# Four tile pairs of each FFN up projection computed by seven half-size products, with the residual kept in DRAM meanwhile

## The chip, the cores and the metric

The kernel runs on one core of a Trainium2 chip. The metric is device time in microseconds (us) of one execution. Engines are named as in the profile: PE (TensorE products), PEld (its weight loads), DVE (VectorE), ACT (ScalarE), POOL (GpSimd) and SP (SyncE, which here only issues DMAs).

## The reference

The reference is an encoder trunk of four layers over x of 512 tokens by 1024 channels, in float32. Each layer is a token mixer (a convolution module, a 2-D neighbourhood attention, a bidirectional retention, and the convolution module again) followed by a gated FFN with a depthwise convolution over tokens. Both are residual. The FFN is what the change touches:

```python
FFN_DIM = ((8 * D_MODEL // 3 + 127) // 128) * 128        # 2816 = 22 * 128

def conv_ffn(h, w_up, dw_w, dw_b, w_down):
    u = dwconv(h @ w_up, dw_w, dw_b)                      # w_up: 1024 x 5632, dwconv: 3 taps
    val, gate = jnp.split(u, 2, axis=-1)
    return (jax.nn.gelu(gate) * val) @ w_down             # w_down: 2816 x 1024

h = rmsnorm(x, norm2_g[i])
x = x + conv_ffn(h, ffn_w_up[i], ffn_dw_w[i], ffn_dw_b[i], ffn_w_down[i])
```

## The kernel before

Activations lie with channels on the partitions: x is eight tiles `x[k]` of 128 channels x 512 tokens, resident in SBUF. For float32 accuracy each operand of a product is split into a high and a low part of the fast format (`split`, `split_w`: a cast on ACT, then a subtraction on DVE), and each product is three (`mm3`, lines 178 to 181: high by high, high by low, low by high). Weights stream from DRAM on the SP queue into two raw buffers (`wraw`), and are split into three high and three low buffers (`whi`, `wlo`).

The four FFNs are `ffn(l, after)`, each in these steps:

- **Up.** The 44 output tiles of 128 channels come as 22 pairs: tile n = 2j is value tile j, n = 2j + 1 is gate tile j. `up(n)` makes one in one PSUM bank: 8 channel tiles x 3 products = 24 products of 128 x 128 weights by 512 tokens. The odd tiles in `ACC` get the low part of their weights by an accumulating DMA on POOL instead of DVE (`load_w_acc`), and have their products on lines 307, 308 and 312.
- **Scaling.** The first tiles use unscaled x. When the norm's statistics are known (after tile `S2[l]`), `scale_first` writes x * gain * rstd into eight temporaries `xs` (line 331), and after tile `SCALED[l] - 1` `scale_rest` splits them anew into `xhi`, `xlo`, which the later tiles read.
- **Middle.** `mid(j)` applies the three taps (lines 349 to 353), the gelu and the gate product. Of pairs below 16 each two channel tiles and the two token halves of 256 make seven combinations `F` (lines 372 to 378), split into `Hh`, `Hl`; pairs 16 to 21 stay plain.
- **Down.** For pairs 0 to 7 and 8 to 15 `down` makes, for each two output tiles, seven products with sums of weight blocks in place of eight with the blocks, each over four channel tiles: 84 products of 256 columns. This is a group, four to each half. `weights` makes the sums with a broadcast load, an accumulating DMA on POOL (line 422) and DVE additions. Two half banks are copied to a temporary `s12` on ACT (lines 467, 470); the results go into the residual `x` in SBUF (line 471 by DMA, lines 473, 476, 454 on DVE). A group's last two products (`finish`) come after the next group's first five, or after the up tiles of the next pair.
- **Rest.** `down_rest` adds pairs 16 to 21 by plain products and finishes `x[o]` (line 292), on which the next mixer starts.

Temporaries `t512` rotate through a pool of `NT_FFN` = 9 tiles. Each engine runs its own instructions in a fixed order, which a scheduler with a timing model lays out when the kernel is built, from the order of the program; so neighbouring up tiles may interleave on PE. DMAs from one engine are issued in that order too.

Of the kernel before, what the change touches and what calls it, by code (L numbers as in the profile page):

```python
# [8 lines left out]
F32 = mybir.dt.float32  # L9
F32R = mybir.dt.float32r  # L10
I32 = mybir.dt.int32
AF = mybir.ActivationFunctionType
# [5 lines left out]
P = 128  # L18
T = 512
D = 1024  # L20
# [51 lines left out]
PART_COL = (0, 2048)  # L72
REST = 16
SLOT_H = 4
NT_FFN = 9
NWS = 3
SCALED = (5, 7, 5, 5)
ACC = tuple(n for n in range(3, 2 * FT, 2) if n // 2 not in (8, 9, 16, 17))


@with_exitstack
def tile_trunk(
# [1 line left out]
    tc: tile.TileContext,  # L84
    xT, par, cos, sin, nmask, rel,
    cw_in, cdw, cdb, cw_out, nat_qkv, rpb, nat_out,
    ret_qk, ret_v, ret_g, ret_out, f_up, f_down, f_rest,
    out,
):
    nc = tc.nc  # L90
# [9 lines left out]
    def nm(s):  # L100
        uid[0] += 1
        return f"{s}{uid[0]}"
# [38 lines left out]
    def pc(name, i=0, w=1):  # L141
        c = COLS[name] + i
        if c < 64:
            return png[:, c:c + w]
        return pt[:, c:c + w]
# [81 lines left out]
                ps[:, b * P:(b + 1) * P], col[:, b:b + 1].broadcast_to([P, P]), ident)  # L227

    state = {"late": [], "squares": []}

    @contextmanager
    def behind(*names):
# [61 lines left out]
    def ffn(l, after):  # L294
        with ExitStack() as st:
# [23 lines left out]
                    scale_rest()  # L319
                return ps  # L320

            xs = []

            def scale_first():
                if SCALED[l] > 2 * FT:
                    return
                for tag in ("Hh0", "Hl0", "Hh1"):
                    t = hp.tile([P, 7, 256], F32, tag=tag, name=nm("xs")).rearrange("p a b -> p (a b)")
                    xs.extend(t[:, i * T:(i + 1) * T] for i in range(3))
                for k in range(KD):  # L330
                    nc.vector.scalar_tensor_tensor(
                        xs[k], x[k], pc("n2g", l * 8 + k), rstd_bc, MUL, MUL)

            def scale_rest():
                for k in range(KD):
                    split(xs[k], xhi[k], xlo[k])

            H, rest, cur_f = {}, {}, {}

# [69 lines left out]
                    state["spare"] = spare  # L409
                return pss  # L410

            def weights(i, q, gate=None):
                p0, p1 = PARTS[q]
                n, c = (p1 - p0) * P, PART_COL[q]
                src = f_down[l, i]
                r13 = hp.tile([P, D], F32, tag="ws", name=nm("ws"), bufs=NWS)
                sg = hp.tile([P, D], F32, tag="wq", name=nm("wq"))
                with tc.issue_after(gate.ins) if gate else ExitStack():
                    nc.sync.dma_start(
                        r13[:, :2 * n].rearrange("p (b n) -> p b n", b=2),  # L420
                        src[:, c + 2 * n:c + 3 * n].unsqueeze(1).broadcast_to([P, 2, n]))
                    nc.gpsimd.dma_start(r13[:, :2 * n], src[:, c:c + 2 * n], accum_op=ADD)
                    r1 = load_raw(src[:, c:c + 2 * n], 2 * n)
                    nc.sync.dma_start(sg[:, n:2 * n], src[:, c + 3 * n:c + 4 * n])
                w1 = split_w(r1, 2 * n, nc.vector)
                w13 = split_w(r13, 2 * n, nc.vector)
                r2 = r13[:, n:2 * n]
                nc.vector.tensor_tensor(r2, r2, r1[:, :n], ADD)
                h2 = hp.tile([P, T], F32R, tag="h2", name=nm("h2"))
                l2 = hp.tile([P, T], F32R, tag="l2", name=nm("l2"))  # L430
                split(r2, h2[:, :n], l2[:, :n])
                nc.vector.tensor_tensor(sg[:, :n], r2, sg[:, n:2 * n], ADD)
                h4 = hp.tile([P, D], F32R, tag="h4", name=nm("h4"))
                l4 = hp.tile([P, D], F32R, tag="l4", name=nm("l4"))
                split(sg[:, :2 * n], h4[:, :2 * n], l4[:, :2 * n])
                u = lambda w, b: (w[0][:, b * n:(b + 1) * n], w[1][:, b * n:(b + 1) * n])
                return {"a11": u(w1, 0), "a22": u(w1, 1), "s3": u(w13, 0), "s1": u(w13, 1),
                        "s2": u((h2, l2), 0), "sg": u((h4, l4), 0), "a12": u((h4, l4), 1)}

            def prod(o, w, q, b, start, stop=True, part=None):  # L440
                p0, p1 = PARTS[q]
                for p in part or range(p0, p1):
                    s = slice((p - p0) * P, (p - p0 + 1) * P)
                    hi, lo = H[p]
                    mm3(o, w[0][:, s], w[1][:, s], hi[:, b, :], lo[:, b, :],
                        start and p == p0, stop and p == p1 - 1, True)

            def down(q, first, late, filler):
                p0, p1 = PARTS[q]

                def finish(i, w, v, s12):
                    prod(v[:, :256], w["sg"], q, 2, False)
                    prod(v[:, 256:], w["a12"], q, 3, True)
                    nc.vector.tensor_tensor(x[2 * i + 1], v, s12, ADD)

                prev = None
                for i in range(4):
                    w = weights(i, q) if i else first
# [8 lines left out]
                    nc.scalar.copy(s12[:, 256:], xc)  # L467
                    prod(v[:, 256:], w["a22"], q, 6, True, part=now)
                    prod(xc, w["s2"], q, 0, False)
                    nc.scalar.copy(s12[:, :256], xc)  # L470
                    nc.gpsimd.dma_start(s12, x[2 * i + 1], accum_op=ADD)
                    prod(v[:, :256], w["s1"], q, 4, True)
                    nc.vector.tensor_tensor(x[2 * i], x[2 * i], v, SUB)
                    prod(xc, w["s3"], q, 5, False)
                    xh2 = x[2 * i].rearrange("p (h t) -> p h t", h=2)
                    nc.vector.tensor_tensor(
                        xh2, xh2, xc.unsqueeze(1).broadcast_to([P, 2, 256]), SUB)
# [41 lines left out]
                    after(o)  # L519

            ups = up_first()
            done, n = 0, 2

            def mids(upto):
                nonlocal done
                while done < upto:
                    for _ in mid(done, ups[2 * done], ups[2 * done + 1]):
                        pass
                    done += 1

            def ups_of(j):
                nonlocal n
                while n < 2 * j + 2:
                    ups.append(up(n))
                    n += 1

            starts = {2 * p1 + (l == 1 and q == 0): q for q, (_, p1) in enumerate(PARTS)}
            for j in range(1, FT):
                ups_of(j)
                w0 = weights(0, starts[j], state["load"]) if j in starts else None  # L540
                if n > S2[l]:
                    mids(j)
                if w0:
                    down(starts[j], w0, lambda: mids(j + 1), lambda: ups_of(j + 1))
            mids(FT)
            state["sq"] = nc.vector
            down_rest()
            del state["sq"]
# [645 lines left out]
                        pair_wout(pss, 3, o2, y3)  # L1194

    def nat_bias():
        dram = ctx.enter_context(
            tc.tile_pool(name="dram", bufs=1, space=bass.MemoryType.DRAM))
# [82 lines left out]
def _layout(inp):  # L1281
# [67 lines left out]
    rw = f["ret_w_in"][0]  # L1349
    rv = rw[:, 2048:4096].reshape(4, 2, P, 4, 512).transpose(3, 0, 2, 1, 4)  # L1350
    rout = f["ret_w_out"][0].reshape(4, 4, P, 4, 2, P).transpose(0, 3, 2, 4, 1, 5)
    fd = f["ffn_w_down"].reshape(4, FT, P, 8, P)
    macros = []
    for i in range(4):
# [22 lines left out]
        "ret_g": tiles(rw[:, 4096:]),  # L1377
        "ret_out": rout.reshape(4, 4, P, D),
        "f_up": tiles(f["ffn_w_up"]),
        "f_down": fdown,  # L1380
        "f_rest": frest,
    }
# [19 lines left out]
```

## Time and profile before

| | |
|---|---|
| median of 3 runs | 2552.09 us (2547.99 to 2552.65) |
| the profiled execution: own time | 2553.76 us |
| its span in the trace | 2552.0 us |
| granted PE clock, mean | 0.997 |
| instructions | 36973 |
| 212 to 549 us, most of the first FFN: PE / DVE / ACT / POOL busy | 336.6 / 215.9 / 163.6 / 45.4 of 337 us |
| the same for 830 to 1160 us, most of the second | 329.9 / 220.2 / 167.3 / 39.1 of 330 us |
| DMA in the whole run | 341.21 MB, 134 GB/s on average |

A profile row by line gives: line, engine, operation, output<-input, shapes, count | busy us, mean ns of one | idle time of the engine just before such instructions, and what ended it. A timeline row gives start, duration, engine, line, and in brackets the idle time before it. Matmuls overlap in the pipeline, so their pace is read from the distance of their starts, not from their listed duration.

### The profile page before, as it was taken

The page shows a single profiled execution, that of the slowest core. Times are in us where ns is not written, and L with a number is a line of the kernel's source. Part 1 is how long each engine was busy: PE and PEld are TensorE (multiplying, and loading weights), DVE is VectorE, ACT ScalarE, POOL GpSimd, SP SyncE. Part 2 cuts the span into 40 slices and gives each one's busy share as a digit, 9 for nine tenths or more (in the row PEclk, how much of TensorE's full clock was granted, in tenths as well). Part 3 has the DMA queues.
Part 4 walks back from the last instruction along what each step waited for, and adds up shares of the span by engine and source line. Part 5 has one row for each costly group of instructions (what it writes and reads, how often), then busy time and mean ns, then how long its engine had stood idle before and what let it go on. Part 6 is the DMA issues. An engine that isn't in the chain of part 4 may idle for free.

```text
span 2552.0 us, 36973 instructions
## 1 busy us (share of the span) xinstructions
PE 2531.0 (99%) x14590; PEld 2158.3 (85%) x14590; DVE 1737.3 (68%) x2828; ACT 1215.1 (48%) x1635; POOL 342.5 (13%) x412
## 2 busy tenths in 40 slices
PE   9999999999999999999999999999999999999999
PEld 7888898979998888888888888889898888789897
DVE  7976766667877676656666565677575887676664
ACT  5454544454656555444332423454444445454442
POOL 1214010003421210100000000200000121100000
PEclk9999999999999999999999999999999999999999
DMA  7725757534232565653222222475754572475653
GB/s 244 233 75 172 178 136 175 139 101 119 81 93 82 131 176 143 171 131 112 82 81 68 84 76 67 114 177 129 183 130 110 203 225 74 115 181 133 177 136 107
DMA packets 107903, 341.21 MB, mean 134 GB/s; under 512 B 13345, under 2 KB 16289, under 8 KB 107729
## 3 DMA queue, kind: packets, MB, share of 16 engines
q1 hardware_dynamic: 81856, 264.72, 33.9%
q0 software_dynamic: 24576, 71.41, 14.9%
q10 hardware_dynamic: 1296, 2.72, 0.3%
q8 instruction: 114, 1.87, 0.3%
q14 instruction: 61, 0.49, 0.1%
HBM read 321.00 MB, written 5.63 MB: 128 GB/s over the span
## 4 chain that ended last, share of the span: by engine, by line
PE 92%; DVE 4%; DMA 2%; ACT 1%; issue 1%; SPq 0%; DVEq 0%; ACTq 0%
PE ps L180 21%; PE ps L179 21%; PE ps L181 21%; PE ps L312 5%; PE ps L308 5%; PE ps L307 5%; PE ps L184 3%; PE ps L186 3%; PE ps L185 3%; DMA wr<-in_f_down 1%; PE ps L665 1%; PE ps L664 1%; PE ps L663 1%; PE ps L400 1%; PE ps L405 1%
## 5 line engine op out<-in xcount | busy, mean ns | idle before, releaser
L165 ACT CAST wh<-wr 128x1024 fp32r<-128x1024 f32 (+1 forms) x310 | 318.2, 1028 | 548.2 <-PE ps L180 204.6
L166 DVE TENSOR_TENSOR wl<-wr,wh 128x1024 fp32r<-128x1024 f32 (+1 forms) x307 | 371.4, 1210 | 231.2 <-ACT wh L165 170.9
L180 PE MATMUL ps<-xl,wh 128*128 128x512 f32 x1312 | 520.3, 397 | 0.3 <-DVE xl L249 0.3
L179 PE MATMUL ps<-xh,wh 128*128 128x512 f32 x1312 | 518.1, 396 | 1.0 <-ACT wh L165 1.0
L181 PE MATMUL ps<-xh,wl 128*128 128x512 f32 x1312 | 516.9, 395 | 0.1
L179 PEld LDWEIGHTS ps<-xh,wh 128*128 128x128 f32 x1312 | 246.3, 188 | 61.7 <-ACT wh L165 1.8
L181 PEld LDWEIGHTS ps<-xh,wl 128*128 128x128 f32 x1312 | 246.3, 188 | 59.2 <-DVE wl L166 0.5
L180 PEld LDWEIGHTS ps<-xl,wh 128*128 128x128 f32 x1312 | 246.4, 188 | 57.7 <-DVE xl L249 0.6
L180 PE MATMUL ps<-Hl,wh 128*128 128x256 f32 (+1 forms) x734 | 224.4, 307 | 1.1 <-DVE Hl L190 1.0
L179 PE MATMUL ps<-Hh,wh 128*128 128x256 f32 (+1 forms) x734 | 223.2, 306 | 0.0
L181 PE MATMUL ps<-Hh,wl 128*128 128x256 f32 (+1 forms) x734 | 222.7, 307 | 0.1
L307 PE MATMUL ps<-xh,wh 128*128 128x512 f32 x544 | 215.1, 395 | 0.0
L308 PE MATMUL ps<-xl,wh 128*128 128x512 f32 x544 | 214.9, 395 | 0.0
L351 DVE SCALAR_TENSOR_TENSOR t<-ps,par,t 128x511 f32<-128x511 f32 x154 | 114.8, 746 | 143.3 <-ACT t L349 143.3
L184 PE MATMUL ps<-wh,xh 128*128 128x256 f32 (+1 forms) x512 | 159.5, 314 | 2.0 <-DVE x L505 2.0
L186 PE MATMUL ps<-wh,xl 128*128 128x256 f32 (+1 forms) x512 | 159.9, 313 | 0.0
L185 PE MATMUL ps<-wl,xh 128*128 128x256 f32 (+1 forms) x512 | 159.6, 313 | 0.0
L175 POOL DMA_DIRECT2D wl<-in_f_up x68 | 59.8, 879 | 665.4 <-ACT wl L174 539.9
L180 PEld LDWEIGHTS ps<-Hl,wh 128*128 128x128 f32 x734 | 138.2, 188 | 9.5 <-DVE Hl L190 1.7
L181 PEld LDWEIGHTS ps<-Hh,wl 128*128 128x128 f32 x734 | 137.5, 188 | 8.9 <-DVE wl L166 1.8
L179 PEld LDWEIGHTS ps<-Hh,wh 128*128 128x128 f32 x734 | 137.7, 188 | 7.7
L312 PE MATMUL ps<-xh,wl 128*128 128x512 f32 x544 | 137.8, 395 | 0.0
(298 smaller groups left out, 5463.5 us busy)
## 6 DMA issues: line engine op xcount, KB each, us to landing
wr<-in_f_up SPq DMA_DIRECT2D x176, 512.0 KB, 4.0
wl<-in_f_up POOLq DMA_DIRECT2D x68, 512.0 KB, 6.6
wraw<-in_cdw SPq DMA_DIRECT2D x56, 608.0 KB, 5.0
ws<-in_f_down SPq DMA_DIRECT2D x32, 512.0 KB, 6.7
wr<-in_f_down SPq DMA_DIRECT2D x32, 512.0 KB, 6.3
ws<-in_f_down POOLq DMA_DIRECT2D x32, 512.0 KB, 8.3
wr<-in_cw_in SPq DMA_DIRECT2D x30, 512.0 KB, 4.1
wr<-in_f_rest SPq DMA_DIRECT2D x32, 384.0 KB, 3.2
```

What stands on the lines that cost most here:

```text
L165: nc.scalar.copy(hi[:, :n], raw[:, :n])
L166: eng.tensor_tensor(lo[:, :n], raw[:, :n], hi[:, :n].bitcast(F32), SUB)
L179: nc.tensor.matmul(o, wh, ah, start=first, stop=False, skip_group_check=free)
L180: nc.tensor.matmul(o, wh, al, start=False, stop=False, skip_group_check=free)
L181: nc.tensor.matmul(o, wl, ah, start=False, stop=last, skip_group_check=free)
L184: nc.tensor.matmul(o, ah, wh, start=first, stop=False)
L185: nc.tensor.matmul(o, ah, wl, start=False, stop=False)
L186: nc.tensor.matmul(o, al, wh, start=False, stop=last)
L307: nc.tensor.matmul(ps, wh[:, s], xhi[k], start=k == 0, stop=False)
L308: nc.tensor.matmul(ps, wh[:, s], xlo[k], start=False, stop=False)
L312: nc.tensor.matmul(ps, wl[:, k * P:(k + 1) * P], xhi[k], start=False, stop=k == KD - 1)
L351: state["mid"] = nc.vector.scalar_tensor_tensor(a[:, 1:], u[:, :T - 1], pt[:, w:w + 1], a[:, 1:], MUL, ADD)
```

## The change

Four pairs of each FFN (`UPS`: 10, 12, 18, 19; in the second FFN 11, 13, 18, 19) are no longer made by two calls of `up` but by `up_macro`, which uses the seven products of the down groups: the blocks are the value and gate tile by even and odd channel tiles, and even and odd channel tiles by token halves. Their weights come from a new array `f_us`, through the split halves of the old `weights` (`sums`, which starts a pair ahead, and `weights`). The token combinations (`combos`) are made once per FFN, one channel pair after each of pairs 4 to 7. Their split parts take the place of `x[k]` in SBUF. So the residual is stored to DRAM tiles `xd` at the FFN's start, the scaling works in place in `x`, the down groups accumulate into `xd` by DMAs on POOL, and `x` is loaded again ahead of `down_rest`. Temporaries go from 9 to 7, and the descriptor scratch of the DMAs is halved.

```diff
-NT_FFN = 9
+NT_FFN = 7
+UPS = ((10, 12, 18, 19), (11, 13, 18, 19), (10, 12, 18, 19), (10, 12, 18, 19))
+COMBO = (4, 5, 6, 7)
...
+    xd = [dram.tile([P, T], F32, tag=f"xd{k}", name=f"xd{k}") for k in range(KD)]
...
-            xs = []
-
             def scale_first():
-                if SCALED[l] > 2 * FT:
-                    return
-                for tag in ("Hh0", "Hl0", "Hh1"):
-                    t = hp.tile([P, 7, 256], F32, tag=tag, name=nm("xs")).rearrange("p a b -> p (a b)")
-                    xs.extend(t[:, i * T:(i + 1) * T] for i in range(3))
                 for k in range(KD):
                     nc.vector.scalar_tensor_tensor(
-                        xs[k], x[k], pc("n2g", l * 8 + k), rstd_bc, MUL, MUL)
+                        x[k], x[k], pc("n2g", l * 8 + k), rstd_bc, MUL, MUL)
 
             def scale_rest():
                 for k in range(KD):
-                    split(xs[k], xhi[k], xlo[k])
+                    split(x[k], xhi[k], xlo[k])
+
+            ch, cl = {}, {}
+
+            def combos(p):
+                e, o = x[2 * p], x[2 * p + 1]
+                c = hp.tile([P, D], F32, tag="ws", name=nm("cx"), bufs=NWS)
+                q = [c[:, i * 256:(i + 1) * 256] for i in range(4)]
+                nc.vector.tensor_tensor(q[0], e[:, 256:], e[:, :256], SUB)
+                nc.vector.tensor_tensor(q[1], o[:, :256], e[:, :256], SUB)
+                nc.vector.scalar_tensor_tensor(q[2], o[:, :256], -1.0, q[0], MUL, SUB)
+                nc.vector.scalar_tensor_tensor(q[3], q[2], -1.0, o[:, 256:], MUL, SUB)
+                cl[p] = hp.tile([P, D], F32R, tag=f"cl{p}", name=nm("cl"))
+                for k, h in ((2 * p, slice(0, T)), (2 * p + 1, slice(T, D))):
+                    ch[k] = const.tile([P, T], F32R, tag=f"x{k}", name=nm("ch"))
+                    split(c[:, h], ch[k], cl[p][:, h])
...
+            open_macro, ahead = [], {}
+
+            def uprod(o, w, b, start, stop=True):
+                for p in range(4):
+                    s = slice(p * P, (p + 1) * P)
+                    mm3(o, w[0][:, s], w[1][:, s], *xblock(p, b),
+                        start and p == 0, stop and p == 3, True)
+
+            def finish_up():
+                if open_macro:
+                    w, v, s12 = open_macro.pop()
+                    uprod(v[:, :256], w["sg"], 2, False)
+                    uprod(v[:, 256:], w["a12"], 3, True)
+                    nc.vector.tensor_tensor(s12, v, s12, ADD)
+
+            def up_macro(j):
+                w = weights(*ahead.pop(j))
+                xb, v = bank(psa), bank(psa)
+                xc = xb[:, :256]
+                s12, u2 = t512(), t512()
+                uprod(xc, w["a11"], 1, True)
+                nc.scalar.copy(s12[:, 256:], xc)
+                uprod(v[:, 256:], w["a22"], 6, True)
+                uprod(xc, w["s2"], 0, False)
+                nc.scalar.copy(s12[:, :256], xc)
+                uprod(v[:, :256], w["s1"], 4, True)
+                uprod(xc, w["s3"], 5, False)
+                finish_up()
+                nc.scalar.activation(u2.rearrange("p (h t) -> p h t", h=2),
+                                     xc.unsqueeze(1).broadcast_to([P, 2, 256]), AF.Copy, scale=-1.0)
+                nc.vector.tensor_tensor(u2, u2, v, SUB)
+                open_macro.append((w, v, s12))
+                return [s12, u2]
...
+            def sums(src, gate=None):
...
+                    nc.gpsimd.dma_start(r13[:, :2 * n], src[:, :2 * n], accum_op=ADD)
+                    nc.sync.dma_start(sg[:, n:2 * n], src[:, 3 * n:])
+                return src, r13, sg
...
                 def finish(i, w, v, s12):
...
-                    nc.vector.tensor_tensor(x[2 * i + 1], v, s12, ADD)
+                    nc.vector.tensor_tensor(s12, v, s12, ADD)
+                    nc.gpsimd.dma_start(xd[2 * i + 1], s12, accum_op=ADD)
...
-                    nc.gpsimd.dma_start(s12, x[2 * i + 1], accum_op=ADD)
                     prod(v[:, :256], w["s1"], q, 4, True)
-                    nc.vector.tensor_tensor(x[2 * i], x[2 * i], v, SUB)
                     prod(xc, w["s3"], q, 5, False)
-                    xh2 = x[2 * i].rearrange("p (h t) -> p h t", h=2)
-                    nc.vector.tensor_tensor(
-                        xh2, xh2, xc.unsqueeze(1).broadcast_to([P, 2, 256]), SUB)
+                    u2 = t512()
+                    nc.scalar.activation(u2.rearrange("p (h t) -> p h t", h=2),
+                                         xc.unsqueeze(1).broadcast_to([P, 2, 256]), AF.Copy, scale=-1.0)
+                    nc.vector.tensor_tensor(u2, u2, v, SUB)
+                    nc.gpsimd.dma_start(xd[2 * i], u2, accum_op=ADD)
...
             ups = up_first()
+            for k in range(KD):
+                nc.sync.dma_start(xd[k], x[k])
...
             def ups_of(j):
                 nonlocal n
+                fetch_sums(j + 1)
+                if j in UPS[l]:
+                    ups.extend(up_macro(j))
+                    n += 2
                 while n < 2 * j + 2:
                     ups.append(up(n))
+                    finish_up()
                     n += 1
+                if j in COMBO:
+                    combos(COMBO.index(j))
...
             mids(FT)
+            for k in range(KD):
+                x[k] = const.tile([P, T], F32, tag=f"x{k}", name=nm("x"))
+                nc.gpsimd.dma_start(x[k], xd[k])
...
-    nc = bacc.Bacc("TRN2", target_bir_lowering=False, num_devices=1, dynamic_dma_scratch_size=8192)
+    nc = bacc.Bacc("TRN2", target_bir_lowering=False, num_devices=1, dynamic_dma_scratch_size=4096)
```

More of the change, by code (lines that the diff above doesn't have):

```diff
@@ L86, in tile_trunk @@
     cw_in, cdw, cdb, cw_out, nat_qkv, rpb, nat_out,
-    ret_qk, ret_v, ret_g, ret_out, f_up, f_down, f_rest,
+    ret_qk, ret_v, ret_g, ret_out, f_up, f_us, f_down, f_rest,
     out,
@@ L229, in tile_trunk @@
     state = {"late": [], "squares": []}
+    dram = ctx.enter_context(tc.tile_pool(name="dram", bufs=1, space=bass.MemoryType.DRAM))
+    xd = [dram.tile([P, T], F32, tag=f"xd{k}", name=f"xd{k}") for k in range(KD)]
     @contextmanager
@@ new lines, in xblock @@
+            def xblock(p, b):
+                if b in (1, 2, 3):
+                    k, c = 2 * p + (b > 1), slice(256 * (b % 2), 256 * (b % 2) + 256)
+                    return xhi[k][:, c], xlo[k][:, c]
+                i = {4: 0, 5: 1, 0: 2, 6: 3}[b]
+                return (ch[2 * p + i // 2][:, i % 2 * 256:i % 2 * 256 + 256],
+                        cl[p][:, i * 256:(i + 1) * 256])
+            open_macro, ahead = [], {}
[4 more added lines that the diff above has]
+                        start and p == 0, stop and p == 3, True)
@@ L410, in up_first @@
                 return pss
[L412 to L415, printed above, removed]
+            def sums(src, gate=None):
+                n = src.shape[-1] // 4
                 r13 = hp.tile([P, D], F32, tag="ws", name=nm("ws"), bufs=NWS)
@@ L420, in weights @@
                         r13[:, :2 * n].rearrange("p (b n) -> p b n", b=2),
[L421 to L424, printed above, removed]
+                        src[:, 2 * n:3 * n].unsqueeze(1).broadcast_to([P, 2, n]))
+                    nc.gpsimd.dma_start(r13[:, :2 * n], src[:, :2 * n], accum_op=ADD)
+                    nc.sync.dma_start(sg[:, n:2 * n], src[:, 3 * n:])
+                return src, r13, sg
+            def weights(src, r13, sg):
+                n = src.shape[-1] // 4
+                r1 = load_raw(src[:, :2 * n], 2 * n)
                 w1 = split_w(r1, 2 * n, nc.vector)
@@ L438, in weights, with down_w @@
                         "s2": u((h2, l2), 0), "sg": u((h4, l4), 0), "a12": u((h4, l4), 1)}
+            def down_w(i, q, gate=None):
+                p0, p1 = PARTS[q]
+                c = PART_COL[q]
+                return weights(*sums(f_down[l, i][:, c:c + 4 * (p1 - p0) * P], gate))
             def prod(o, w, q, b, start, stop=True, part=None):
@@ L453, in finish @@
                     prod(v[:, 256:], w["a12"], q, 3, True)
-                    nc.vector.tensor_tensor(x[2 * i + 1], v, s12, ADD)
+                    nc.vector.tensor_tensor(s12, v, s12, ADD)
+                    nc.gpsimd.dma_start(xd[2 * i + 1], s12, accum_op=ADD)
                 prev = None
                 for i in range(4):
-                    w = weights(i, q) if i else first
+                    w = down_w(i, q) if i else first
                     xb, v = bank(psa), bank(psa)
@@ L529, in mids, with fetch_sums @@
                     done += 1
+            def fetch_sums(j):
+                if j in UPS[l]:
+                    ahead[j] = sums(f_us[l, UPS[l].index(j)], state["load"])
             def ups_of(j):
                 nonlocal n
+                fetch_sums(j + 1)
+                if j in UPS[l]:
+                    ups.extend(up_macro(j))
+                    n += 2
                 while n < 2 * j + 2:
                     ups.append(up(n))
+                    finish_up()
                     n += 1
+                if j in COMBO:
+                    combos(COMBO.index(j))
             starts = {2 * p1 + (l == 1 and q == 0): q for q, (_, p1) in enumerate(PARTS)}
@@ L539, in ffn @@
                 ups_of(j)
-                w0 = weights(0, starts[j], state["load"]) if j in starts else None
+                w0 = down_w(0, starts[j], state["load"]) if j in starts else None
                 if n > S2[l]:
@@ L1196, in nat_bias @@
     def nat_bias():
-        dram = ctx.enter_context(
-            tc.tile_pool(name="dram", bufs=1, space=bass.MemoryType.DRAM))
         gp = dram.tile([NH, 8, 504], F32, tag="gp", name="gp")
@@ L1351, in _layout @@
     rout = f["ret_w_out"][0].reshape(4, 4, P, 4, 2, P).transpose(0, 3, 2, 4, 1, 5)
+    fu = f["ffn_w_up"].reshape(4, 4, 2, P, 44, P)
+    fus = np.stack([np.stack([np.concatenate(
+        [fu[l, :, par, :, j + c].transpose(1, 0, 2).reshape(P, T)
+         for c, par in ((0, 0), (FT, 1), (FT, 0), (0, 1))], -1) for j in UPS[l]]) for l in range(DEPTH)])
     fd = f["ffn_w_down"].reshape(4, FT, P, 8, P)
@@ L1379, in _layout @@
         "f_up": tiles(f["ffn_w_up"]),
+        "f_us": fus,
         "f_down": fdown,
```

## The prediction

> **What bounds the kernel now.** I read the page first: busy shares, granted clock, and the chain that ended last.
>
> ```profile
> span 2552.0 us, 36973 instructions
> PE 2531.0 (99%) x14590; PEld 2158.3 (85%) x14590; DVE 1737.3 (68%) x2828; ACT 1215.1 (48%) x1635; POOL 342.5 (13%) x412
> PEclk9999999999999999999999999999999999999999
> PE 92%; DVE 4%; DMA 2%; ACT 1%; issue 1%; SPq 0%; DVEq 0%; ACTq 0%
> ```
>
> PE is idle for 2552.0 - 2531.0 = 21.0 us in all, at full granted clock, and is 92% of the chain. Time goes only if matrix work goes. A busy PE can hide slow pacing, so I next looked at pace: the chain in order of time for the up stage, and ACT's timeline for the down stage, which already uses seven-product groups.
>
> ```profile
> 384.13 1.87 PE ps L312 x8
> 395.33 1.87 PE ps L312 x8
> 406.53 1.87 PE ps L312 x8
> ...
> 330.97 0.38 ACT L467 COPY t<-ps 128x256 f32<-128x256 f32 x1 [0.37 <-PE ps L181]
> 340.98 0.37 ACT L467 COPY t<-ps 128x256 f32<-128x256 f32 x1 [0.49 <-PE ps L181]
> ```
>
> The first three rows are the tail of each odd up tile: one pair of tiles every 11.20 us. It holds 2 x 24 = 48 products of 512 columns, so 11.20 / 48 = 0.2333 us each. The other two are the same copy in successive down groups: 10.01 us for 7 x 4 x 3 = 84 products of 256 columns, 0.1192 us each.
>
> Last, who makes PE wait (the waits of PE over the whole span; only these two rows name a tile of the FFN's middle).
>
> ```profile
> PE ps L180 <- DVE Hl L190: 1.0, 2, 0.7
> PE ps L179 <- ACT wh L165: 1.0, 2, 0.8
> ```
>
> **The change part by part.**
>
> *PE.* 16 pairs (4 in each of 4 FFNs) go from 48 long to 84 short products: 16 x (11.20 - 10.01) = 19.0 us saved. That is the whole gain.
>
> A page speaks against it. The Trainium skill (TensorE: Matmul & The Clock Gate, section Back-to-back issue gap) gives about 81 ns per product at 128 columns and 131 ns at 512 in a stream of load and product pairs; a straight line puts 256 columns at 98 ns, an estimate from that page. By it a pair would go from 6.3 to 8.2 us and the change would cost 16 x 1.9 = 31 us. The trace does not agree: 233 and 119 ns.
>
> *DVE and ACT in such a pair.* Grouped by line and shape:
>
> ```profile
> L166 DVE TENSOR_TENSOR wl<-wr,wh 128x1024 fp32r<-128x1024 f32 x275 | 340.8, 1239 | 204.4 <-ACT wh L165 161.6 <-PE ps L312 40.1 <-issue 1.4
> L165 ACT CAST wh<-wr 128x1024 fp32r<-128x1024 f32 x278 | 291.8, 1050 | 491.4 <-PE ps L180 176.2 <-issue 148.4 <-PE ps L186 56.8
> L428 DVE TENSOR_TENSOR ws<-ws,wr 128x512 f32<-128x512 f32 x32 | 22.0, 689 | 0.5
> L189 ACT CAST h<-ws 128x512 fp32r<-128x512 f32 x32 | 19.9, 621 | 43.9 <-DVE ws L428 29.0 <-PE ps L181 11.9 <-PE ps L180 2.9
> L476 DVE TENSOR_TENSOR x<-x,ps 128x512 f32<-128x512 f32 x32 | 21.9, 683 | 1.5
> L349 ACT ACTIVATE t<-ps,par 128x512 f32<-128x512 f32 x154 | 117.9, 773 | 39.1 <-PE ps L312 38.9
> L377 DVE SCALAR_TENSOR_TENSOR F<-F 128x256 f32<-128x256 f32 x32 | 13.5, 423 | 0.8
> ```
>
> DVE gains three full-width splits (3 x 1.24), three half-width steps (sum, its split, second sum: 3 x 0.69) and two evacuations (2 x 0.69), and loses the even tile's split (1.24): 3.72 + 2.07 + 1.38 - 1.24 = +5.9 us. ACT gains three casts, one half cast, two 0.37 copies and one negated copy (0.77, as L349) and loses three full-width passes: 3.15 + 0.62 + 0.74 + 0.77 - 3.15 = +2.1 us. The four token combinations of each FFN each cost DVE 4 x 0.42 + 2 x 0.69 = 3.1 us and ACT 2 x 0.62 = 1.2 us. In the down groups a DVE subtraction of 0.68 becomes an ACT copy of 0.77, eight times per FFN. Sum per FFN: DVE 4 x 5.9 + 4 x 3.1 - 8 x 0.68 = +30.6 us, ACT +19.6 us.
>
> Does it fit under PE? Busy time by stretch (PE, PEld, DVE, ACT, POOL, clock, DMA share, GB/s):
>
> ```profile
> 372.00:395.00 23.00, 23.00 (x101) 18.48 (x100) 12.06 (x17) 11.62 (x14) 2.63 (x3) 1.00 0.60 142
> 395.00:417.00 22.00, 22.00 (x96) 17.71 (x95) 12.78 (x16) 11.36 (x14) 1.74 (x2) 1.00 0.60 141
> 440.00:462.00 22.00, 22.00 (x179) 21.63 (x178) 18.64 (x22) 11.61 (x17) 2.62 (x3) 1.00 0.67 166
> 484.00:502.00 18.00, 18.00 (x91) 15.02 (x90) 7.28 (x10) 8.95 (x11) 1.75 (x2) 1.00 0.42 112
> 502.00:524.00 22.00, 22.00 (x96) 17.71 (x95) 10.65 (x15) 11.52 (x14) 1.53 (x2) 1.00 0.59 135
> ```
>
> Pairs 10 to 13 lie in the first two rows: DVE 24.8 us of 45. Two of the four change: 24.8 + 11.8 = 36.6 us under 45 - 2.4 = 42.6 us of PE, 86%. The down stretch of the third row ran at 18.64 / 22 = 85% with PE never waiting. Pairs 18 and 19 adjoin: 10.65 + 11.8 = 22.4 us of DVE against 20.0 of PE. The excess of 2.4 us is covered by the idle DVE before it (18 - 7.28 = 10.7 us), where weights can be split ahead; without that cover it costs 2.4 x 4 = 10 us in all.
>
> *Handing PSUM over.* In each new group PE may not add to a half bank until ACT has copied it; twelve products of another bank (1.43 us) stand between. The copy takes 0.37 us, and the down rows above show ACT waiting for PE. In the up stage ACT also carries the middle's work. The wait lies between 0 and, if one full cast and one half-bank copy are ahead in ACT's order, 1.05 + 0.37 + 0.37 - 1.43 = 0.4 us; twice in 16 groups that is 0 to 13 us. I take 0.05 us each, 1.6 us in all, because the instruction order is laid out around such waits and PE's listed ones are under 1 us.
>
> *Down start.* The third combination falls before the first down group, where the one wait on Hl was 0.7 us at most. DVE's 3.1 us go into its idle time there or in front of Hl: 0 to 3.1 us, four times, 0 to 12 us. I take 0.35 each, 1.4 us: DVE is half idle there:
>
> ```profile
> 295.00:305.00 10.00, 10.00 (x44) 8.05 (x43) 2.90 (x4) 2.78 (x4) 1.73 (x2) 1.00 1.07 302
> ```
>
> *Residual in DRAM.* Eight stores of 256 KB are added on SP at each FFN's start, and scaling, now in place, must wait for them. Issues (KB, us to landing), then SP, DVE and PE in order of time:
>
> ```profile
> out<-x SPq DMA_DIRECT2D x7, 256.0 KB, 2.0
> t<-x POOLq DMA_DIRECT2D x32, 256.0 KB, 4.8
> ws<-in_f_down SPq DMA_DIRECT2D x32, 512.0 KB, 6.7
> ws<-in_f_down POOLq DMA_DIRECT2D x32, 512.0 KB, 8.3
> ...
> 206.60 5.93 SPq L156 DMA_DIRECT2D wr<-in_f_up  x2
> 222.15 2.53 SPq L156 DMA_DIRECT2D wr<-in_f_up  x2
> ...
> 210.05 0.69 DVE L734 TENSOR_TENSOR x<-ps,x 128x512 f32<-128x512 f32 x1 [2.81 <-PE ps L181]
> 229.57 5.39 DVE L331 SCALAR_TENSOR_TENSOR xs<-x,png,rstd_bc 128x512 f32<-128x512 f32 x8 [3.39 <-ACT rstd_bc L281]
> 235.49 1.29 DVE L190 TENSOR_TENSOR xl<-xs,xh 128x512 fp32r<-128x512 f32 x2
> ...
> 238.75 0.39 PE L307 MATMUL ps<-xh,wh 128*128 128x512 f32 x1
> ...
> 205.00:215.00 10.00, 10.00 (x45) 8.04 (x44) 4.61 (x6) 3.66 (x6) 4.09 (x3) 1.00 0.33 99
> 225.00:235.00 10.00, 10.00 (x46) 8.09 (x45) 6.41 (x15) 4.25 (x6) 5.83 (x11) 1.00 0.96 284
> ```
>
> The last x is ready at 210.7; SP issues nothing from 212.5 to 222.1 while the DMA engines are a third busy. Eight issues of 0.33 us and 2 MB at the spare 200 GB/s take about 10 us, so they land by about 222, before scaling starts at 229.57. I cost them at nothing; cover 7 us. In the down groups the sums now go to DRAM (64 accumulating transfers instead of 32 into SBUF); nobody waits for one but the eight reloads. Those follow the last accumulating up load on POOL (first and last start, then DVE):
>
> ```profile
> L156 SPq DMA_DIRECT2D wr<-in_f_up x176: 327/328/384, 191.4 to 2488.7; - x176
> L175 POOL DMA_DIRECT2D wl<-in_f_up x68: 863/874/987, 223.9 to 2500.1; - x68
> 2526.06 1.40 DVE L292 TENSOR_TENSOR x<-ps,x 128x512 f32<-128x512 f32 x2 [5.91 <-PE ps L181]
> ```
>
> Free at 2501, eight issues of 0.87 us end at 2508, plus 4.8 us is 2513, against first use at 2526: 13 us of cover. While POOL waits for a broadcast load (6.7 us) or a sum, later accumulating loads queue behind it. The lead is long: 48 products (11.2 us) lie between the up stage's end and 2526.1, so its last tile starts at 2509.3, 20.6 us after its load was issued at 2488.7. A new group's sums are released by the load of the last tile before the preceding pair, 20.6 + 5.6 + 11.2 = 37 us ahead, against a chain of 6.7 + 0.9 + 8.3 us and 4 us of splitting, 20 us. I cost that at nothing too, at most 2 us a group. Traffic per FFN rises by 2 MB of stores, 2 MB net of accumulation, 2 MB of reloads and 1 MB of weights, 28 MB in all, at DMA shares near 0.6. Fewer temporaries (7 for 9) and half the descriptor scratch delay only engines with idle time: 0 to 2 us, taken as 0.
>
> *Sum.* -19.0 + 1.6 + 1.4 = -16.0 us. The profiled execution took 2553.8 (span 2552.0 and 1.8 around it): it would take 2537.8. The median is 1.7 us lower: 2536.1.
>
> **The rivals.**
>
> *Handovers and DVE eat much of it.* Handovers at 0.2 us (32 x 0.2 = 6.4), pairs 18 and 19 uncovered by half (5) and the down start at 0.35 (1.4) cost 12.8: -6.2 us, 2546. For: DVE at 86% and 112% in these pairs. Against: no wait of PE in the 85% stretch.
>
> *Late stores hold back scaling: slower.* If the stores stand behind the up loads on SP, they begin at about 224 and meet the 0.96 DMA share of the last row above. At some 100 GB/s left they take 20 us and land at 244; scaling starts 14.5 us late. The first split (235.49 + 0.65) is 2.6 us ahead of its product at 238.75, so PE stalls 12 us per FFN: 48 - 16 = +32 us, 2584. It decides from a stall of 16.0 / 4 = 4 us per FFN, stores landing after about 236. Against: SP's free 10 us, and this share was seen in the first FFN only, so I think it takes at most one FFN usually.
>
> *Short products pay per product, not per column.* Were each bound by its weight load as listed,
>
> ```profile
> L180 PEld LDWEIGHTS ps<-xl,wh 128*128 128x128 f32 x1312 | 246.4, 188 | 57.7 <-DVE xl L249 0.6
> ```
>
> 84 x 0.188 = 15.8 us a pair, 16 x 4.6 = +74 us, 2626. The down groups, same shape and loads, show 10.01. The page's 31 us would come of the same cause.
>
> *It does nothing visible.* Handovers at their 13 us, and 3 us each for the excess at pairs 18 and 19 and the down start: 0, 2552.
>
> **How the numbers follow.** Forecast 0.66, reaching from no stalls (2533.1) to 6 us of them (2539); handovers and DVE 0.18 (2539 to 2547); nothing visible 0.07; late stores 0.08; per product 0.01. The first two make faster by over 0.2% (5.1 us, about what a measurement of this kernel tells from no change) 0.84; same 0.07; slower 0.09. The range 2532 to 2546 holds the forecast and most of the second case, about 8 in 10; its lower end allows 1 us of scatter between runs.
>
> **What would show it.** Right: PE about 19 us less busy, 576 products more, the group period 10.0 us in the new pairs, idle PE below 26 us, scaling starting where it did relative to the first products. Wrong: PE waits on a copied half bank, on Hl or on weights of the new groups totalling over 10 us; scaling waiting for the stores; PE's busy time not falling.

## The result and the profile after

The changed kernel takes 2618.45 us (median of 6 runs, 2614.92 to 2619.92) against 2550.54 us (6 runs): ratio 1.0265, 95% interval 1.0251 to 1.0278. It is 68 us slower, where 16 us faster was forecast. First its page: span, busy times, shares of the chain that ended last.

```profile
span 2617.6 us, 38827 instructions
PE 2543.1 (97%) x15166; PEld 2192.1 (84%) x15166; DVE 1824.9 (70%) x3004; ACT 1264.4 (48%) x1763; POOL 393.9 (15%) x484
PE 80%; DMA 8%; DVE 7%; ACT 3%; issue 2%; POOL 0%; DVEq 0%; SPq 0%; ACTq 0%; POOLq 0%
```

The span grew by 65.6 us. PE is idle for 2617.6 - 2543.1 = 74.5 us, 53.5 more than before. It is also busy for 12.1 us more, although 576 more but shorter products should have made it 19 us less: some 31 us went into slower products. DMA went from 2% of the chain to 8%. Who makes PE wait, in the waits of PE over the span:

```profile
PE ps L183 <- DVE wl L168: 20.4, 13, 3.5
PE ps L181 <- DVE t L538: 15.2, 4, 4.2
PE ps L182 <- DVE Hl L192: 5.6, 7, 1.1
PE ps L316 <- DMA wl<-in_f_up: 5.3, 3, 4.5
```

Before, the FFN's middle had 2.0 us of waits. The second row (four waits, one in each FFN) names the subtraction that reads bank v (line 538), which here was the last in a queue. The timeline before one of them shows what held it:

```profile
482.90 0.33 SPq L475 DMA_DIRECT2D wq<-in_f_down  x1
...
493.80 0.69 DVE L488 TENSOR_TENSOR wq<-ws,wq 128x512 f32<-128x512 f32 x1 [9.61 <-DMA wq<-in_f_down]
...
494.66 1.04 ACT L191 CAST h<-wq 128x1024 fp32r<-128x1024 f32 x1 [10.56 <-DVE wq L488]
...
498.01 0.68 DVE L538 TENSOR_TENSOR t<-t,ps 128x512 f32<-128x512 f32 x1
...
498.75 0.38 PE L181 MATMUL ps<-Hh,h 128*128 128x256 f32 x1 [4.20 <-DVE t L538]
```

A load of 256 KB is issued at 482.90, when the last reader of the single tile `wq` has ended (482.88), and lands at 493.7. DVE stands idle for it for 9.61 us, ACT for 10.56, everything queued on both comes late, and PE stalls for 4.20 us. Sorted by place, some 25 us of PE's gaps in the FFNs lie at pairs 18 and 19, behind late `wq` loads such as this one, and some 17 us at the start of the second down half. Busy time by stretch shows both places (columns as in the prediction):

```profile
440.00:450.00 10.00, 6.74 (x42) 6.04 (x41) 7.64 (x10) 2.27 (x2) 0.86 (x1) 0.83 0.59 139
480.00:490.00 10.00, 10.00 (x68) 9.17 (x67) 4.10 (x5) 2.05 (x3) 2.62 (x3) 1.00 1.00 213
490.00:500.00 10.00, 5.80 (x34) 4.96 (x33) 5.55 (x8) 3.83 (x6) 1.71 (x2) 0.98 0.67 130
500.00:510.00 10.00, 8.62 (x61) 8.42 (x61) 6.33 (x9) 4.73 (x7) 0.03 (x1) 0.85 0.46 107
1080.00:1090.00 10.00, 5.87 (x27) 5.00 (x26) 8.15 (x9) 3.09 (x3) 0.87 (x1) 0.66 0.61 141
```

The first and last row are starts of the second down half, in the first and second FFN. The load of 482.90 fell into the second row, where the DMA engines were 1.00 busy. The granted clock of 0.66 to 0.85 beside the stalls is where most of the other 31 us went. Starts of PE's products after the stall:

```profile
499.09 0.28 PE L183 MATMUL ps<-Hh,l 128*128 128x256 f32 x1
...
499.21 0.28 PE L181 MATMUL ps<-Hh,h 128*128 128x256 f32 x1
...
499.56 0.41 PE L181 MATMUL ps<-Hh,h 128*128 128x256 f32 x1
...
499.77 0.42 PE L182 MATMUL ps<-Hl,h 128*128 128x256 f32 x1
```

Products start 0.12 us apart, then 0.21 until 503.0. Such stretches of half clock (3.41 to 10.24 us each) add up to 54.5 us in the FFNs of this execution: at half pace, some 27 us lost (an estimate: half of 54.5). Before, the FFNs had none.

The traffic also differs from the 28 MB expected. Bytes moved, from the changed kernel's page, and below it its issues of the new pairs' weights:

```profile
DMA packets 128521, 381.18 MB, mean 146 GB/s; under 512 B 15521, under 2 KB 18465, under 8 KB 128337
```
```profile
ws<-in_f_us SPq DMA_DIRECT2D x24, 512.0 KB, 7.3
...
wr<-in_f_us SPq DMA_DIRECT2D x16, 512.0 KB, 8.3
```

381.18 - 341.21 = 40.0 MB. And `ws` is loaded 24 times for 16 new pairs (`wr` 16 times): eight sets of sums are loaded and never read. `ups_of` is called twice for the pair after each down half, once to fill the half's end and once by the loop, and each call asks for the next pair's sums.

### The profile page after: what moved, and what is told of

It reads as the page before. It is cut to its first block, busy times and chain, and to the rows that moved or that the text cites. A ratio compares the mean times of both kernels' runs of the same rounds, so it can differ in the third digit from the quotient of the medians.

```text
span 2617.6 us, 38827 instructions
## 1 busy us (share of the span) xinstructions
PE 2543.1 (97%) x15166; PEld 2192.1 (84%) x15166; DVE 1824.9 (70%) x3004; ACT 1264.4 (48%) x1763; POOL 393.9 (15%) x484
## 2 busy tenths in 40 slices
DMA packets 128521, 381.18 MB, mean 146 GB/s; under 512 B 15521, under 2 KB 18465, under 8 KB 128337
## 4 chain that ended last, share of the span: by engine, by line
PE 80%; DMA 8%; DVE 7%; ACT 3%; issue 2%; POOL 0%; DVEq 0%; SPq 0%; ACTq 0%; POOLq 0%
PE ps L182 19%; PE ps L183 19%; PE ps L181 19%; PE ps L316 3%; PE ps L312 3%; PE ps L311 3%; PE ps L187 3%; PE ps L186 3%; PE ps L188 3%; DMA wr<-in_f_down 2%; DMA wq<-in_f_us 2%; DVE wl L168 2%; DMA wq<-in_f_down 2%; DMA wl<-in_f_up 1%; PE ps L743 1%
## 5 line engine op out<-in xcount | busy, mean ns | idle before, releaser
L183 PE MATMUL ps<-xh,wl 128*128 128x512 f32 (+1 forms) x1248 | 486.4, 391 | 11.6 <-DVE wl L168 11.6
L182 PE MATMUL ps<-xl,wh 128*128 128x512 f32 (+1 forms) x1248 | 488.2, 391 | 0.3 <-DVE xl L253 0.3
L181 PE MATMUL ps<-xh,wh 128*128 128x512 f32 (+1 forms) x1248 | 486.1, 390 | 0.8 <-ACT wh L167 0.8
L183 PEld LDWEIGHTS ps<-xh,wl 128*128 128x128 f32 x1248 | 235.2, 189 | 67.1 <-DVE wl L168 15.2
L181 PEld LDWEIGHTS ps<-xh,wh 128*128 128x128 f32 x1248 | 235.2, 189 | 54.7 <-ACT wh L167 1.7
L311 PE MATMUL ps<-xh,wh 128*128 128x512 f32 x416 | 164.7, 396 | 1.3 <-ACT wh L175 1.3
L312 PE MATMUL ps<-xl,wh 128*128 128x512 f32 x416 | 164.4, 395 | 0.0
L488 DVE TENSOR_TENSOR wq<-ws,wq 128x512 f32<-128x512 f32 x48 | 33.1, 689 | 138.8 <-DMA wq<-in_f_down 94.3
L181 PE MATMUL ps<-Hh,h 128*128 128x256 f32 x384 | 111.7, 291 | 15.7 <-DVE t L538 15.2
L316 PE MATMUL ps<-xh,wl 128*128 128x512 f32 x416 | 107.9, 401 | 5.3 <-DMA wl<-in_f_up 5.3
```

The costliest lines, as they stand in the source:

```text
L181: nc.tensor.matmul(o, wh, ah, start=first, stop=False, skip_group_check=free)
L182: nc.tensor.matmul(o, wh, al, start=False, stop=False, skip_group_check=free)
L183: nc.tensor.matmul(o, wl, ah, start=False, stop=last, skip_group_check=free)
L311: nc.tensor.matmul(ps, wh[:, s], xhi[k], start=k == 0, stop=False)
L312: nc.tensor.matmul(ps, wh[:, s], xlo[k], start=False, stop=False)
L316: nc.tensor.matmul(ps, wl[:, k * P:(k + 1) * P], xhi[k], start=False, stop=k == KD - 1)
```

## The experiments

The theories, in the letters of the expectations: **A**, weight loads come late (A': the new loads meet those of the down groups). **B**, DVE has too much work in the new pairs (B': it is bunched before the second down half). **C**, the residual in DRAM costs time. **D**, formed on the way: `finish_up` adds into bank v, which a DVE subtraction still has to read, and the change put that read behind s3 (line 388, and line 538 in the down groups), where the down groups had read v straight after s1. All times are medians beside runs of the kernel before on the same chip (2549.5 to 2550.5).

**Parts of the change.** e1 keeps the DRAM residual, the scaling in place, seven temporaries and the halved scratch, and has no new pair. e2 has the first two new pairs of each FFN, e3 the last two.

```diff
+LAYOUT = <the old UPS, for the weight array>
-UPS = ((10, 12, 18, 19), (11, 13, 18, 19), (10, 12, 18, 19), (10, 12, 18, 19))
+UPS = ((),) * 4   # e1, with COMBO = ();   e2: ((10, 12), (11, 13), (10, 12), (10, 12));   e3: ((18, 19),) * 4
```

> Keeps the residual in DRAM, the in-place scaling, the 7 temporaries and the half scratch; no pair uses seven products and no combinations are made. Theory A (the loss comes from the weight loads of the new pairs: they crowd the DMA queues, loads on which DVE and ACT wait in their fixed order land late, PE stalls and its clock drops): within 12 us of before, 2550 to 2562. Theory B (DVE has too much work in and around the new pairs): the same, 2550 to 2560. Theory C (the residual in DRAM, its accumulating transfers and the smaller buffers cost it): 2590 or more.

> Only the first two new pairs of each FFN (10 and 12, or 11 and 13), with all four combinations. The trace of the changed kernel has 17 us of PE waits at the start of the second down half, behind a late Hl, and about 10 us lost to the clock there. Theory A: the waits at that start remain, those of pairs 18 and 19 go: 2565 to 2580. Theory B: half of the DVE work, half of the loss or more: 2575 to 2600. Theory C: 2600 or more.

> Only pairs 18 and 19 of each FFN. The changed kernel has about 26 us of PE waits that go back to a late load of the sums' second half (tile wq), nearly all there. Theory A: 2572 to 2592. Theory B: DVE has 22.4 us of work under 20.0 of PE there but idles before, so 2550 to 2575. Theory C: 2600 or more.

Measured: e1 2551.13, ratio 1.0005 [0.9995, 1.0014]; e2 2588.56, 1.0155 [1.0139, 1.0170]; e3 2581.78, 1.0124 [1.0109, 1.0139]. C falls: e1 moves 366.40 MB, 25 MB more than before, for nothing. The harm is in the new pairs, and either half of them does harm. Neither A nor B fits both halves: e2 lies in B's range and 9 us above A's, e3 in A's and 7 us above B's.

**Two `wq` tiles**, alone (e4), with the last two pairs (e5), and with three (e6: 10 or 11, 18, 19).

```diff
-sg = hp.tile([P, D], F32, tag="wq", name=nm("wq"))
+sg = hp.tile([P, D], F32, tag="wq", name=nm("wq"), bufs=2)
```

> The changed kernel with two buffers for the tile wq in place of one, so that its load can be issued a group earlier; work and traffic are the same. Theory A: DVE's holds of about 10 us on wq go, and with them some 26 us of PE waits and their share of the clock loss, 10 us: 2575 to 2592. Theory B and C: no change, 2610 to 2622.

> Two wq buffers and only pairs 18 and 19 of each FFN. Theory A (late loads behind the single wq did the harm there): PE's saving of 9.5 us comes through, 2540 to 2550. Theory B (DVE has too much work there): 2555 to 2580, little better than with one buffer.

> Two wq buffers, the new pairs 10 (11 in the second FFN), 18 and 19. Theory B' (what is left with two buffers, some 30 us, is DVE's work of the new pairs 10 and 12 bunched in front of the second down half): one pair and two plain ones behind it leave time to catch up, 2538 to 2552. Theory A' (what is left is the loads of the new pairs meeting those of the down half): half of it stays, 2555 to 2570.

Measured: e4 2582.01, 1.0127 [1.0112, 1.0143]; e5 2560.52, 1.0044 [1.0029, 1.0059]; e6 2558.17, 1.0031 [1.0019, 1.0043]. The late loads are worth 36 us, but 32 are left above before. So what this mends is about half of the loss. e5 lies in the range of B, e6 in that of A', so neither explains what is left.

**Reading v early.** e7 has two `wq` tiles and, in `up_macro` and in `down`, this; e9 has it with one `wq`; e10 with two, in `up_macro` alone (`u2h` is u2 seen as two halves of 256 columns):

```diff
 uprod(v[:, :256], w["s1"], 4, True)
+nc.scalar.activation(u2, v, AF.Copy, scale=-1.0)
 uprod(xc, w["s3"], 5, False)
 finish_up()
-nc.scalar.activation(u2.rearrange(...), xc.unsqueeze(1).broadcast_to([P, 2, 256]), AF.Copy, scale=-1.0)
-nc.vector.tensor_tensor(u2, u2, v, SUB)
+nc.vector.tensor_tensor(u2h, u2h, xc.unsqueeze(1).broadcast_to([P, 2, 256]), SUB)
```

> All new pairs, two wq buffers; the temporary u2 is now the negated copy of the bank v, taken before the last product of the group, and DVE subtracts the half bank xc from it afterwards, so that PE need not wait for DVE before it adds to v again. If that order makes PE wait by itself: 8 to 15 us less than with two wq buffers alone, 2566 to 2574. If those waits were only the late wq passed on: 2577 to 2585.

> The changed kernel with the negation of bank v taken first, in the new pairs and in the down groups, and one wq buffer as it was. If the late wq load and the order of the subtraction cost it independently (36 us and 34 us by the earlier runs): 2580 to 2588. If the subtraction's order is the root, and the late wq only hurt because the groups were drawn out by it: 2548 to 2565.

> Two wq buffers, the negation first in the new pairs alone; the down groups subtract as in the changed kernel. If the harm sits in the new pairs, whose last two products the program's order put behind another tile: 2547 to 2558. If it sits in the down groups, where the listed waits on the subtraction are: 2570 to 2582.

Measured: e7 2547.47, 0.9995 [0.9985, 1.0004]; e9 2558.34, 1.0030 [1.0021, 1.0040]; e10 2550.55, 1.0005 [0.9995, 1.0014]. Alone the early read gives 60 us, beside two `wq` 35, and 31 of these in the new pairs. e7 is 19 us below both of its ranges: the order cost far more than the listed waits on the subtraction. e9 and e10 lie in the ranges in which the order, and that in the new pairs, is the root.

**Less work for DVE.** e8 has two `wq` tiles and leaves out the low parts of five of seven weight blocks in the new pairs (another block's low part is used); e16 does the same in e11 (below).

```diff
-w = weights(*ahead.pop(j))
+w = weights(*ahead.pop(j), low=False)   # r13, r2 and sg: only the cast, w1's low part for theirs
```

> All new pairs, two wq buffers, and in the new pairs the low parts of five of the seven weight blocks are left out (the low part of another block is used in their place), which takes 3.1 us from DVE per new pair and leaves loads, products and their order of need. Theory B': the waits at the second down half shrink with DVE's work, 2550 to 2567. Theory A': no change, 2576 to 2585.

> The fastest kernel so far (two tiles wq, negated copy first, gate), and in the new pairs the low parts of five of seven weight blocks are left out: another block's low part is used in their place, so PE does the same products and DVE has some 3.1 us less in each of 16 pairs. Theory B (DVE's amount of work still costs): 2528 or less. Theory D (with the reads in order DVE has time enough): 2531 to 2536. If dropping the low parts itself does harm, as it seemed to in the kernel with two tiles wq alone (22 us slower), by holding the first low buffer until the pair is finished: 2545 or more.

Measured: e8 2604.05, 1.0213 [1.0196, 1.0231], 22 us slower than e4; e16 2533.28, 0.9935 [0.9919, 0.9952], the same as e11. First the engines' row of e16, then that of e11:

```profile
PE 2510.7 (99%) x15166; PEld 2172.7 (86%) x15166; DVE 1791.7 (71%) x2956; ACT 1274.9 (50%) x1763; POOL 395.2 (16%) x484
```
```profile
PE 2509.1 (99%) x15166; PEld 2171.5 (86%) x15166; DVE 1834.4 (72%) x3004; ACT 1275.0 (50%) x1763; POOL 395.6 (16%) x484
```

43 us less DVE work bring nothing once v is read early: B falls there. With the late read e8 cannot test B, as it missed both ranges by a loss of its own. Most of that sits in one row of its waits of PE:

```profile
PE ps L183 <- DVE l L192: 14.4, 5, 4.3
```

Four of these are 3.0 to 4.3 us, one in each FFN, and each leads back to a `wq` load of the new pairs that landed late. Why that load was issued later than in e4 stays open.

**The queue order.** In e7 the raw weights of a half's first group stood on SP behind the sums of groups 1 and 2. A gate holds the sums of each of groups 1 to 3 back until the raw weights of the group before it are issued (the last load that `state["load"]` names at that point, so not the last up load, as one of the expectations below has it):

```diff
-w = down_w(i, q) if i else first
+w = down_w(i, q, state["load"]) if i else first
```

e11 is e7 with it, e12 is e11 with `NT_FFN = 9`, e13 the gate alone, e14 gate and two `wq`, e15 gate and early read.

> Two wq buffers, negation first everywhere, and each down group's sums may be loaded only once the raw weights of the group before it have been issued, so that SP no longer sends the sums of three groups ahead of the first group's raw weights. If PE's waits left at the down starts (1 to 2 us each, behind raw weights that land 13 us after their issue) come of that order: 2535 to 2544, below before. If they come of the amount of traffic: 2545 to 2551.

> As the kernel before it, with nine temporaries in place of seven. If the two temporaries fewer hold up ACT's taps: 3 to 8 us less than the kernel before it. If they do not: within 3 us of it.

> The changed kernel with one edit: the sums of a half's groups 1 to 3 wait for the last up load, as those of group 0 do, so the raw weights of group 0 stand ahead of them on the SP queue. One tile wq, and the subtraction that reads v only after s3, as in the changed kernel. Theory A (late weight loads are the cause, the order of reading matters only through them): most of the 68 us goes, 2565 or less. Theory D (the subtraction of v after s3 is the cause, in the new pairs; the loads come second): the gate can give back what it gave beside the two other edits, about 14 us, 2600 to 2610.

> The changed kernel with two tiles wq and the same gate, so that both delays of the loads are mended, but v still read only after s3. Theory A: 2533 to 2540, as the kernel with all three edits. Theory D: 2582 less at most 14, that is 2565 to 2580, with the stalls at the second down half's start still there.

> The negated copy of v straight after s1, and the gate, with one tile wq. Theory D: near the kernel with all three edits, 2533 to 2545, since negation alone gave 60 us. Theory A in a weaker form (the single tile wq costs some 11 us whenever v is read early): 2544 to 2550.

Measured: e11 2533.28, 0.9934 [0.9921, 0.9946], faster than both kernels; e12 2533.94, 0.9935 [0.9922, 0.9949]; e13 2608.42, 1.0228 [1.0213, 1.0244]; e14 2566.12, 1.0064 [1.0049, 1.0079]; e15 2552.31, 1.0010 [1.0001, 1.0020]. e11 is 2 us below its lower range; e13 and e14 are where D has them; e15 missed D's range by 7 us and the weaker A's by 2, so something about the single `wq` was still unexplained. All eight combinations:

| us | v read after s3 | v read before s3 | difference |
|---|---|---|---|
| one `wq` | 2618.45 | 2558.34 | 60 |
| one `wq`, gate | 2608.42 | 2552.31 | 56 |
| two `wq` | 2582.01 | 2547.47 | 35 |
| two `wq`, gate | 2566.12 | 2533.28 | 33 |

The early read gives most in e9 and still 33 us where the loads are mended; the second `wq` gives 36 and 42 us where v is read late, 11 and 19 where it is read early; the gate 6 to 16. e14 and e11 differ in the read alone. Of each, in order of time, the first new pair of the first FFN, from ACT's first copy to DVE's finished sum. e14:

```profile
363.64 0.36 ACT L379 COPY t<-ps 128x256 f32<-128x256 f32 x1
...
375.77 0.59 ACT L386 ACTIVATE t<-ps 128x512 f32<-128x512 f32 x1
...
377.04 0.68 DVE L388 TENSOR_TENSOR t<-t,ps 128x512 f32<-128x512 f32 x1
...
384.22 0.69 DVE L371 TENSOR_TENSOR t<-ps,t 128x512 f32<-128x512 f32 x1
```

e11:

```profile
361.23 0.37 ACT L379 COPY t<-ps 128x256 f32<-128x256 f32 x1 [0.46 <-PE ps L183]
...
364.49 0.58 ACT L384 ACTIVATE t<-ps 128x512 f32<-128x512 f32 x1
...
373.11 0.68 DVE L388 TENSOR_TENSOR t<-t,ps 128x512 f32<-128x512 f32 x1
...
375.64 0.68 DVE L371 TENSOR_TENSOR t<-ps,t 128x512 f32<-128x512 f32 x1
```

Then three stretches of each, e14 first:

```profile
370.00:380.00 10.00, 10.00 (x51) 8.32 (x50) 5.33 (x7) 5.51 (x7) 0.00 (x0) 1.00 0.29 58
...
420.00:430.00 10.00, 10.00 (x44) 8.05 (x43) 10.00 (x13) 4.02 (x6) 0.21 (x2) 1.00 0.87 233
...
440.00:450.00 10.00, 5.48 (x35) 4.87 (x34) 6.24 (x8) 3.00 (x3) 0.86 (x1) 0.90 0.58 127
```
```profile
370.00:380.00 10.00, 10.00 (x62) 8.91 (x61) 9.58 (x13) 6.01 (x6) 0.00 (x0) 1.00 0.12 23
...
420.00:430.00 10.00, 10.00 (x45) 8.04 (x44) 6.94 (x10) 2.99 (x5) 1.56 (x2) 1.00 1.01 280
...
440.00:450.00 10.00, 10.00 (x86) 10.00 (x86) 6.53 (x8) 4.84 (x8) 0.87 (x1) 1.00 0.69 185
```

And from DVE's timeline the low part of the last combination that the second down half needs, e14 first:

```profile
445.35 2.02 DVE L192 TENSOR_TENSOR Hl<-F,Hh 128x1792 fp32r<-128x1792 f32 x1 [1.75 <-ACT Hh L191]
```
```profile
432.87 2.02 DVE L192 TENSOR_TENSOR Hl<-F,Hh 128x1792 fp32r<-128x1792 f32 x1
```

In e14 v is read at 377.04, after s3 and its copy at 375.77; in e11 ACT reads it at 364.49. The pair's results come 20.6 us after the first copy, not 14.4, since the built order puts products of another up tile between s3 and the last two products (in the changed kernel, 22 of them from 375.9 to 381.6). While PE works on that, DVE lacks work (5.33 against 9.58 us in 370 to 380). It does it later: at 420 to 430 it has no idle time (10.00 against 6.94 us), and the last combination starts at 445.35 instead of 432.87. So at 440 to 450, where the second down half starts and needs it, PE is busy for 5.48 us of 10 and the clock drops. D stands.

**The unread sets.** e17 is the changed kernel, e18 is e15, each with the sums asked for once:

```diff
-if j in UPS[l]:
+if j in UPS[l] and j not in ahead:
     ahead[j] = sums(f_us[l, UPS[l].index(j)], state["load"])
```

> The changed kernel issues 24 sets of the new pairs' sums where 16 are read: the up tiles that fill the end of a down half ask for the next pair's sums, and the loop asks again right after; so twice in each FFN a set is loaded, nobody reads it, and it takes a turn of the tile wq, one of three tiles ws and 1.25 MB. This run asks once; nothing else is changed. Theory D (v read after s3 in the new pairs costs most, the weight loads come second): at most what the second tile wq gave, 36 us: 2582 to 2612. If the unread sets are the main cause: 2565 or less. Bytes moved must fall by 10.5 MB to 370.7 in any case.

> The kernel with the negated copy first and the gate, with one tile wq (2552), and the sums asked for once. If a second wq was only needed because unread sets took turns of the one: 2531 to 2540, and the waits for wq go. If one tile is too few by itself: 2545 or more, with the waits of DVE on the wq loads still near 74 and 53 us.

Measured: e17 2578.98, 1.0111 [1.0090, 1.0133], 39 us below the changed kernel with 370.70 MB moved, 3 us below D's range, so the unread sets cost more than D allowed; e18 2534.86, 0.9942 [0.9927, 0.9956], where e15 had 2552. The main rows of e18's waits of PE:

```profile
PE ps L718 <- DVE t L712: 3.8, 2, 1.9
PE ps L186 <- DVE x L567: 2.2, 1, 2.2
```

Both lie outside the FFNs' middle. The wait for a late accumulating load (`wl<-in_f_up`, 5.3 us in the changed kernel) is gone as well. e18 and e11 are equal (2534.86, 2533.28): the second `wq` paid for the unread sets, which took turns of the single tile ahead of sets that were read. DVE still waits for the down groups' `wq` loads in e18 (66.1 us, 73.8 in e15) without holding PE: that part of the expectation failed; its waits for those of the new pairs fell from 52.8 to 4.8 us. So the 84 us between the changed kernel and e18 have three sources, which add to more alone than together: the late read of v (60 us alone), the unread sets (39 us alone), and the queue order (10 us alone). With the queue order beside it, either of the first two suffices to turn the gain into a loss: e9 has only the unread sets left and the order, e17 only the late read and the order.

## Why the prediction was wrong, point by point

- **PE's saving: right.** Kernels with the waits mended have PE busy for 2509.1 (e11), 2510.5 (e18) and 2510.7 us (e16), against 2531.0 - 19.0 = 2512.0. Some 2 to 5 us of these 20 to 22 are clock and not matrix work, an estimate from the mean granted clock of the profiled executions (0.997 before, 0.998 to 0.999 here). The rate of the Trainium skill (TensorE: Matmul & The Clock Gate, section Back-to-back issue gap), by which the change would have cost 31 us, is not borne out here either.
- **Handing PSUM over: the step that failed.** "The wait lies between 0 and [...] 0.4 us; twice in 16 groups" counted only the two half banks that ACT copies. The diff showed a third read: the last two products add into v, and the subtraction of v had moved from before s3 to behind s3, an ACT copy and DVE's queue. That wait was never named, so nobody asked what the built order would put in its place. It was left out of a term taken at 1.6 us and at most 13; the runs price it at 33 to 60 us.
- **The prefetch: the second that failed.** "I cost that at nothing too, at most 2 us a group" took one set for each pair. The two calls of `ups_of` were in the code. They cost 39 us in the changed kernel. The traffic says the same: 25.2 MB for the residual (e1; forecast 24) and 10.5 for unread sets (381.18 - 370.70) leave 4.3 for weights (forecast 4). And "DMA shares near 0.6" was an average over 22 us; in the 10 us that mattered it was 1.00.
- **The queue order** was not in the sum: 6 to 16 us.
- **The clock** was not in the sum: a stall was priced at its own length. Here 53.5 us more idle time came with some 27 us lost to half clock.
- **DVE at pairs 18 and 19, and the down start: right as amounts.** e16 shows that less DVE work gains nothing, and e11 and e18 have no wait over 0.9 us in the FFNs' middle. (DVE's busy time grew by 97 us in e11, where 4 x 30.6 = 122 were forecast: too high, on the safe side.) What the changed kernel lost at the second down half followed from the late read, not from the combinations.
- **Residual in DRAM, temporaries, scratch: right.** e1 and e12 show no cost, and scaling starts at 228.31 in the changed kernel where it started at 229.57. In both kernels DVE waits before it for ACT alone, 14.0 us over the four FFNs, so the rival of late stores did not occur:

```profile
228.31 5.39 DVE L328 SCALAR_TENSOR_TENSOR x<-x,png,rstd_bc 128x512 f32<-128x512 f32 x8 [3.40 <-ACT rstd_bc L285]
```

- **The rivals.** "Handovers and DVE eat much of it" came nearest in place, but stopped at 12.8 us, since it too priced each wait by itself. With the read, the sets and the order mended, e11 and e18 land 16 to 17 us below before, where the sum had put the change. (e11 has the unread sets still and a second `wq` for them.) The gate was not run in the kernel before; its FFNs' middle had only 2.0 us of waits to give.

## What to carry to other kernels

When a group's last products add into a bank, list every engine that still reads that bank and after which product it can; a read that moves behind one more product moves the finish, and the order that is built around it. Count the calls of a prefetch, not the consumers: a set that nobody reads takes a turn of a single buffer, and the next load starts only when that buffer is free, whatever lead its gate gives it. Read the DMA share in stretches as short as a load, and price a PE stall of some microseconds with the slower clock that may follow it.

## What the runs showed of the hardware

The clock falls after shorter stalls than the one at 498.75. PE in the changed kernel, at the start of the second down half:

```profile
444.22 0.39 PE L183 MATMUL ps<-Hh,wl 128*128 128x256 f32 x1 [1.89 <-DVE wl L168]
...
445.54 0.41 PE L181 MATMUL ps<-Hh,wh 128*128 128x256 f32 x1
445.75 0.41 PE L182 MATMUL ps<-Hl,wh 128*128 128x256 f32 x1
```

After 1.89 us of idleness products start 0.21 us apart. A stall of this length does not always do it: outside the FFNs a wait of 1.93 us ends at 133.53 in the changed kernel and one of 1.92 us at 133.03 in e11, and the granted clock from 130 to 136 was 0.86 in the first and 1.00 in the second. The Trainium skill (TensorE: Matmul & The Clock Gate, section What's actually happening) has the clock halved after about one idle window of 3.4 us; the length of the stretches here (3.41 us, or two or three times that) agrees with such a window; the idle time before this one was shorter.

A 256 KB load, issued at 482.90 behind loads of the new pairs' weights, took 10.8 us from issue to landing while the DMA engines were 1.00 busy at 213 GB/s. The median of the 32 loads of its kind was 8.2 us in the changed kernel. Before, the same 32 had this row among the DMA issues (KB, median us to landing):

```profile
wq<-in_f_down SPq DMA_DIRECT2D x32, 256.0 KB, 3.0
```
